# Order edges in a fused decoder step: attention outputs ahead of the output projection's second half, memory and keys turned later

## The chip, the cores and the metric

The kernel runs on one core of a Trainium2 chip. The metric is device time of one execution in microseconds (us). Before the change the median of three runs is 2836.79 us (2836.49 to 2840.41).

Five engines work side by side, each through a list of instructions of its own, in order: TensorE (PE in the profile; its weight loads are PEld), VectorE (DVE), ScalarE (ACT), GpSimd (POOL) and SyncE (SP), which here only issues transfers. They wait for each other by semaphores. A profile also records the clock that TensorE was granted, as a share of full speed (PEclk).

## The reference, cut to what matters

One layer over 2048 prompt tokens of width 1024, and beside it 8 sequences of 4 new tokens. A mixer joins gated linear attention (4 heads) with a spatial gating unit, then come a cross-attention to 256 memory tokens and a gated feed-forward part with a causal convolution; each has an RMS norm ahead and a residual add behind.

```python
def gla_chunked(q, k, v, logg, s0):            # chunks of the sequence
    b = jnp.cumsum(gc, axis=1)
    o = scores @ vc + (qc * jnp.exp(b)) @ S    # outputs: within the chunk, and from the state
    S = jnp.exp(b_last) * S + (kc * jnp.exp(b_last - b)).T @ vc

def mixer(xn, s0, lp):
    ...
    o, S = gla_chunked(q, k, v, logg, s0)
    o = rmsnorm(o, g_gla_out).reshape(B, T, GLA_WIDTH) * jax.nn.silu(r)
    s_out = u * z                              # the gating unit: z mixes positions of sv
    y = jnp.concatenate([o, s_out], axis=-1) @ w_out

def mem_kv(mem, g_mem, wk_x, wv_x):
    mn = rmsnorm(mem, g_mem)
    return mn @ wk_x, mn @ wv_x                # both are outputs too

h = x + mixer(...); h = h + mem_attend(...); out = rmsnorm(h + conv_ffn(...), g_final)
```

(Abridged and partly in short notation.)

## The kernel before, in words

The prompt is worked through in four blocks of 512 tokens, 0 to 3; the new tokens ride along with block 1 in the mixer and with block 2 in the feed-forward part. Products in float32 precision are made from three matmuls (`mm3`: high by high, high by low, low by high), for which every operand is split into a high part (ACT, L84) and a low part (DVE, L85; POOL for some). In names, `h_` and `l_` are the parts of a weight, `ch` and `cl` those of the mixer's output, `r_` a raw weight.

Ahead of block 0 lies the memory stage. `mem_proj` multiplies the normed memory with the key weights and then the value weights, head by head (`mkp`, `mvp`), scales the result into `mkf`/`mvf` on DVE (L568), and at once turns it on TensorE (`mkt`, `mvt`, L577) to store it. Into this stage are woven the turns of block 0's input (`xt`) and of the convolution's state (`sctp`, from transfers `sc`).

In each block, gated linear attention works on two pairs of heads. `decay(p)` makes the decayed keys `kh` (the last step on POOL, L1082) and turns them (`ktp`, L1085); `states(p)` makes the chunk's products `kv` (L1104) and the running state `S` (DVE, L1111); `chunks(p, i)` makes the outputs: `op` (L1127 and L1128, two matmuls per head and chunk, so four for a pair and chunk), copied by DVE (L1129) into `o` for chunk c of 128 tokens. Then, for each c, `onorm(c)` squares (ACT, L1173), sums (DVE, L1174), multiplies by r (L1176) and takes the root through `rt` (DVE, L307) and `ors` (POOL, L308), and `gate(c)` scales (DVE, L1181). `back(h)` turns the result (`otp`, L1187) and splits it into `ch` (ACT, L88) and `cl` (DVE, L89).

The output projection takes eight inputs k: 0 to 3 are linear attention, 4 to 7 the gating unit. With `whole` (blocks 0, 2 and 3) the half over inputs 4 to 7 is made first, for output tiles m = 0 to 3, and these four sums stay open in PSUM as `a_wo`; the matmuls over inputs 0 to 3 follow once `back` is done. Each step of `out_proj_steps` holds two tiles m; the second open step is m = 2 and 3. Block 1 has no open sums.

In block 0 weights are also folded (`qk_steps`, `vo_steps`): `fold_vo` makes `vop` on TensorE and its parts `voh` (ACT) and `vol` (DVE), and stores them for later blocks. `weave` spreads such side steps over steps a to b of the main line; `vo_steps` have (11, 19).

At the very end `last_rows` makes the last rows of the feed-forward part (`dr`), adds them to `ht`, sums squares, and `finish(c, ss)` scales chunk c and stores it; `finish` runs one chunk behind.

What sets the order: the program is written as steps, and a scheduler then sorts each engine's instructions from their dependencies and a model of their times, so an instruction can end up ahead of others that were written before it. A manual dependency of the kind NoSync adds no semaphore; it only keeps one instruction behind another on an engine.

Of the kernel before, what the change touches and what calls it, by code (L numbers as in the profile page):

```python
# [23 lines left out]
SB = 512  # L24
# [13 lines left out]
def hymba_step_kernel(  # L38
# [34 lines left out]
    def mps(name):  # L73
        return mmp.tile([128, 512], F32, tag="mm", name=name)
# [12 lines left out]
    def split_scaled(hi, lo, src, g):  # L87
        act.activation(hi, src, AF.Copy, scale=g)  # L88
        dve.scalar_tensor_tensor(lo, src, g, hi.bitcast(F32), ALU.mult, ALU.subtract)  # L89

    def mm3(ps, wh, wl, xh, xl, first, last):
        pe.matmul(ps, wh, xh, start=first, stop=False)  # L92
        pe.matmul(ps, wh, xl, start=False, stop=False)  # L93
        pe.matmul(ps, wl, xh, start=False, stop=last)  # L94

    def wraw(name):
# [430 lines left out]
    def mem_norm():  # L527
# [27 lines left out]
        mem_st.rs, mem_st.bc = rs, bc  # L555
        mem_st.out, mem_st.t = {}, {}

    def mem_proj(nm, h, od, *ws):

# [10 lines left out]
        for x, t in enumerate((th, tl)):  # L570
            nc.sync.dma_start(kvd[nm, h][:, x], t[:, :512].bitcast(F32))
        if h % 2 == 0:
            mem_st.out[nm] = [U(f"m{nm}o{h}{c}") for c in range(2)]
# [87 lines left out]
    for nm, w, od in (("k", wk_x, o_mem_k), ("v", wv_x, o_mem_v)):  # L661
        od = od[0, 0].rearrange("m h d -> m (h d)")
        for h in range(4):
            mem_steps.append(Step(lambda a, b, nm=nm, h=h, od=od: mem_proj(nm, h, od, a, b),
                                  [(w[0], 4 * j, 4, h * 256, 256, f"w{nm}{h}{j}") for j in range(2)]))
# [278 lines left out]
    def gla_steps(B):  # L944
# [6 lines left out]
        def gates():  # L951
# [24 lines left out]
            B.lg = lg  # L976
            B.P, B.qz, B.kt, B.eb, B.kms, B.b, B.S = {}, {}, {}, {}, {}, {}, {}

# [31 lines left out]
        def level(p, l):  # L1010
# [41 lines left out]
            if sample and l < 2:  # L1052
# [3 lines left out]
                for hh in range(2):  # L1056
                    dst = B.P[2 * p + hh][:NS, SB:TM].rearrange("p (n two h) -> p n two h", two=2, h=half)
                    dve.copy_predicated(dst[:, :, 1, :], masks[l][:NS, :16].rearrange("p (n h) -> p n h", h=half),
                                        ps[:NS, hh * 16:(hh + 1) * 16].rearrange("p (n h) -> p n h", h=half))

        def decay(p):
            e0 = T_(f"e0{s}{p}")
# [19 lines left out]
            pool.tensor_tensor(kh[:, :T], kh[:, :T], B.k[p][:, :T], ALU.mult)  # L1082
            ps = mps(f"ktp{s}{p}")
            for c in range(4):
                pe.transpose(ps[:, c * 128:(c + 1) * 128], kh[:, c * 128:(c + 1) * 128], ident)  # L1085
            t = U(f"kt{s}{p}")
            dve.tensor_copy(t[:, :SB], ps)
            B.kt[p] = t
            if sample:
# [8 lines left out]
        def states(p):  # L1098

            kv = mps(f"kv{s}{p}")  # L1100
            for c in range(4):
# [14 lines left out]
        def chunks(p, i):  # L1116

            if p == 0 and i == 0:
                B.o = [U(f"o{s}{c}") for c in range(nt)]
            ps = mps(f"op{s}{p}{i}")  # L1120
            for j in range(2):
                c = 2 * i + j
                cs = slice(c * 128, (c + 1) * 128)
                for hh in range(2):
                    h = 2 * p + hh
                    os_ = slice(j * 256 + hh * 128, j * 256 + (hh + 1) * 128)
                    pe.matmul(ps[:, os_], B.P[h][:, cs], B.v[c][:, h * 128:(h + 1) * 128], start=True, stop=False)  # L1127
                    pe.matmul(ps[:, os_], B.qz[h][:, cs], B.S[p][c], start=False, stop=True)  # L1128
                dve.tensor_copy(B.o[c][:, p * 256:(p + 1) * 256], ps[:, j * 256:(j + 1) * 256])  # L1129
# [81 lines left out]
    def out_proj_steps(B, unit, src, g, name, sample, first, finished, keep=None, seven=False,  # L1211
# [11 lines left out]
        def half(m2, k0, last, begin=True, end=True):  # L1223

            def fn(wu):
                wh, wl = wu
                x = src()
                if m2 == 0 and last:
                    B.hn, B.sq = [], None
                for mm in range(2):  # L1230
                    m = 2 * m2 + mm
                    ms = slice(mm * 128, (mm + 1) * 128)
                    for ci, (c0, cw) in enumerate(chunks_of(sample)):
                        cs = slice(c0, c0 + cw)
                        ps = acc(f"a_{name}{s}{k0}{m}{ci}") if begin else open_.pop(m)
                        for k in range(4):
                            mm3(ps[:, :cw], wh[:, k, ms], wl[:, k, ms], x[k0 + k][0][:, cs], x[k0 + k][1][:, cs],
                                begin and k == 0, end and k == 3)
                        if end:
# [280 lines left out]
    def ffn_steps(B, last=False):  # L1520
# [110 lines left out]
        def last_rows(*ws):  # L1631
# [8 lines left out]
            def finish(c, ss):  # L1640
                for j in range(2):
# [3 lines left out]
                    else:  # L1645
                        dve.scalar_tensor_tensor(y[:, :512], cur["ht", c, j][:, :512], ss[:, 3:4], gfin[j][:, :512],
                                                 ALU.mult, ALU.mult)
                    nc.sync.dma_start(y_prompt[0, s * SB + c * 128:s * SB + (c + 1) * 128, j * 512:(j + 1) * 512], y[:, :512])

            ready = None  # L1650
            for c in range(4):
                cs = slice(c * 128, (c + 1) * 128)
                ss = narrow(f"yss{s}{c}")
                for j in range(2):
# [6 lines left out]
                    if (c, j) == (3, 1):  # L1661
                        cur["free"], y = y, U("htl")
                        cur["ht", c, j] = y
                        dve.tensor_tensor(y[:, :512], ps, cur["free"][:, :512], ALU.add)
                    else:
# [104 lines left out]
    for s, B in enumerate(blocks):  # L1770
# [6 lines left out]
        if B.mix_sample:  # L1777
            def keep():
                if not hasattr(smp, "x"):
# [63 lines left out]
```

## Time and profile before

| what | us |
|---|---|
| median of 3 runs | 2836.79 |
| the profiled execution | 2837.18 |
| its span | 2835.5 |
| TensorE busy in it | 2797.1 (99%) |
| DVE, ACT, POOL busy | 1894.6, 1106.0, 569.5 |
| mean granted clock of TensorE | 0.995 |
| largest wait of TensorE: otp for the gated o (3 times) | 5.8 |

TensorE is busy nearly throughout. What an order can change is read from the waits of that one engine, from the clock that it had around them, and from the timeline of the other engines just ahead of each wait. In the timeline a row is: start, length, engine, line, operation, output and inputs, count, and in brackets the idle time ahead of it with what ended it.

### The profile page before, as it was taken

How to read it: one execution, taken by the hardware profiler on the slowest of the kernel's cores; microseconds unless marked ns; L12 is line 12 of the kernel's file. 1: busy time of each engine (PE TensorE's matmuls, PEld its weight loads, DVE VectorE, ACT ScalarE, POOL GpSimd, SP SyncE). 2: the span in 40 equal slices, each digit the busy share in tenths (PEclk: the TensorE clock that was granted, in tenths of full speed). 3: DMA queues.
4: the chain of work that ended last, by engine and by line, in shares of the span. 5: the costliest groups of instructions: out<-in, count | busy, mean ns of one | idle time of the engine just before them, and what ended most of it. 6: DMA issues, size and time to landing. Idle time of an engine off the chain costs nothing.

```text
span 2835.5 us, 47052 instructions
## 1 busy us (share of the span) xinstructions
PE 2797.1 (99%) x17894; PEld 2477.9 (87%) x17894; DVE 1894.6 (67%) x3266; ACT 1106.0 (39%) x1950; POOL 569.5 (20%) x638
## 2 busy tenths in 40 slices
PE   8999999999999999999999999999999999999998
PEld 8888888888887898898888889899999888899997
DVE  6578778777657786655555778666666687665555
ACT  5645544333363354223124445422223544431222
POOL 2002213111111221322210121222221022132222
PEclk9999999999999999999999999999999999999999
DMA  9756589999932245888995216577776323677774
GB/s 297 250 182 219 180 267 341 336 343 329 337 112 68 85 154 195 314 288 291 331 324 190 82 60 208 194 252 258 258 269 207 112 69 128 206 260 273 272 281 177
DMA packets 369687, 638.21 MB, mean 225 GB/s; under 512 B 27370, under 2 KB 238412, under 8 KB 369462
## 3 DMA queue, kind: packets, MB, share of 16 engines
q1 hardware_dynamic: 369462, 635.20, 65.7%
q8 instruction: 142, 2.33, 0.3%
q14 instruction: 83, 0.68, 0.1%
HBM read 507.69 MB, written 127.41 MB: 224 GB/s over the span
## 4 chain that ended last, share of the span: by engine, by line
PE 63%; DVE 3%; ACT 1%; issue 0%; POOL 0%; DMA 0%; POOLq 0%; DVEq 0%; ACTq 0%
PE d L94 4%; PE d L92 4%; PE d L93 4%; PE a_wx L94 2%; PE a_wx L93 2%; PE a_wx L92 2%; PE a_wo L92 1%; PE s L1046 1%; PE a_wo L93 1%; PE a_wo L94 1%; PE a_wu L92 1%; PE a_wu L93 1%; PE t_wr L92 1%; PE t_wr L93 1%; PE a_wu L94 1%; PE t_wr L94 1%
## 5 line engine op out<-in xcount | busy, mean ns | idle before, releaser
L92 PE MATMUL d<-acth,whi_wd 128*128 128x272 f32 (+1 forms) x688 | 235.4, 342 | 0.0
L1692 DVE TENSOR_TENSOR h<-d,h 128x512 f32<-128x512 f32 (+1 forms) x232 | 133.7, 582 | 149.4 <-PE d L94 149.2
L94 PE MATMUL d<-acth,wlo_wd 128*128 128x272 f32 (+1 forms) x688 | 233.4, 340 | 0.0
L93 PE MATMUL d<-actl,whi_wd 128*128 128x272 f32 (+1 forms) x688 | 233.3, 339 | 0.0
L1589 POOL TENSOR_TENSOR c<-c,bc_f 128x512 f32<-128x512 f32 (+1 forms) x88 | 137.0, 1562 | 140.4 <-ACT c L1588 139.7
L1579 ACT ACTIVATE c<-g,colsb 128x512 f32<-128x512 f32 x88 | 71.7, 815 | 189.7 <-DVE g L1542 141.7
L94 PEld LDWEIGHTS d<-acth,wlo_wd 128*128 128x128 f32 x688 | 129.5, 188 | 15.5 <-issue 1.2
L93 PEld LDWEIGHTS d<-actl,whi_wd 128*128 128x128 f32 x688 | 129.5, 188 | 13.5 <-issue 0.4
L92 PEld LDWEIGHTS d<-acth,whi_wd 128*128 128x128 f32 x688 | 129.6, 188 | 13.1
L1611 POOL TENSOR_TENSOR c<-r_q_wup,c 128x512 f32<-128x512 f32 (+1 forms) x33 | 63.3, 1918 | 329.4 <-DVE r_q_wup L288 209.6
L92 PE MATMUL a_wo<-ch,h_wo 128*128 128x512 f32 (+1 forms) x320 | 114.3, 369 | 2.0 <-ACT r L876 1.3
L1576 POOL COPY carry<-g 128x2 f32<-128x2 f32 x88 | 29.5, 335 | 420.8 <-DVE g L1542 418.8
L93 PE MATMUL a_wo<-cl,h_wo 128*128 128x512 f32 (+1 forms) x320 | 113.8, 358 | 0.0
L94 PE MATMUL a_wo<-ch,l_wo 128*128 128x512 f32 (+1 forms) x320 | 112.9, 356 | 0.0
L1580 DVE SCALAR_TENSOR_TENSOR c<-g,colsb,c 128x512 f32<-128x512 f32 x88 | 84.9, 965 | 28.3 <-ACT c L1579 27.8
L94 PE MATMUL a_wx<-pTh,wlo_wx 128*128 128x512 f32 x256 | 101.3, 396 | 0.0
L93 PE MATMUL a_wx<-pTl,whi_wx 128*128 128x512 f32 x256 | 100.6, 393 | 0.0
L92 PE MATMUL a_wx<-pTh,whi_wx 128*128 128x512 f32 x256 | 100.2, 394 | 0.0
L84 ACT ACTIVATE acth<-c 128x512 fp32r<-128x512 f32 (+1 forms) x88 | 55.9, 637 | 109.6 <-DVE c L1611 78.0
L1588 ACT ACTIVATE c<-c 128x512 f32<-128x512 f32 (+1 forms) x88 | 56.1, 637 | 94.5 <-DVE c L1581 82.6
L1581 DVE SCALAR_TENSOR_TENSOR c<-g,colsb,c 128x512 f32<-128x512 f32 x88 | 90.6, 1029 | 1.1
L85 DVE TENSOR_TENSOR actl<-c,acth 128x512 fp32r<-128x512 f32 (+1 forms) x88 | 63.1, 720 | 26.6 <-ACT acth L84 25.6
(3753 smaller groups left out, 9741.8 us busy)
## 6 DMA issues: line engine op xcount, KB each, us to landing
whi_wd<-wd SPq DMA_DIRECT2D x66, 512.0 KB, 7.7
wlo_wd<-wd SPq DMA_DIRECT2D x66, 512.0 KB, 7.3
r_wo<-in_w_out_dram SPq DMA_DIRECT2D x32, 512.0 KB, 3.4
wlo_wx<-vod SPq DMA_DIRECT2D x32, 512.0 KB, 4.2
whi_wx<-vod SPq DMA_DIRECT2D x32, 512.0 KB, 5.0
r_wg<-in_w_gate_dram SPq DMA_DIRECT2D x22, 512.0 KB, 7.6
r_wup<-in_w_up_dram SPq DMA_DIRECT2D x22, 512.0 KB, 5.3
r_wd<-in_w_down_dram SPq DMA_DIRECT2D x22, 512.0 KB, 4.5
```

The costliest lines, as they stand in the source:

```text
L84: act.activation(hi, src, AF.Copy)
L85: (lo_eng or dve).tensor_tensor(lo, src, hi.bitcast(F32), ALU.subtract)
L92: pe.matmul(ps, wh, xh, start=first, stop=False)
L93: pe.matmul(ps, wh, xl, start=False, stop=False)
L94: pe.matmul(ps, wl, xh, start=False, stop=last)
L1579: act.activation(c[:, :SB], g[:, 2:SB + 2], AF.Identity, bias=cb, scale=w2)
L1580: dve.scalar_tensor_tensor(c[:, :SB], g[:, 1:SB + 1], w1, c[:, :SB], ALU.mult, ALU.add)
L1581: dve.scalar_tensor_tensor(c[:, :SB], g[:, 0:SB], w0, c[:, :SB], ALU.mult, ALU.add)
L1588: act.activation(c[:, :T], c[:, :T], AF.Gelu_apprx_tanh)
L1589: pool.tensor_tensor(c[:, :T], c[:, :T], B.fbc[:, :T], ALU.mult)
L1611: (dve, pool)[i].tensor_tensor(c[:, :T], q[i], c[:, :T], ALU.mult)
L1692: dve.tensor_tensor(B.h[m + mm][:, cs], ps[:, :cw], B.h[m + mm][:, cs], ALU.add)
```

## The change

Five edits, of which none adds or takes away an operation:

1. `mem_turn`: a head's memory product is turned in the step of the next head (the last one in its own).
2. `keys_turned`: for the second pair of block 0 alone the keys are turned in `states` and no longer in `decay`.
3. `behind(B.last_o, mm)`: the first matmul of the second open step (m = 2, first k) stands behind the last `op` matmul written before it.
4. `behind(cur["added"], out)`: a scaling by DVE in `finish` stands behind the last add, if that add has been written already.
5. `vo_steps` are woven over (11, 17) in place of (11, 19).

```diff
+    in_turn = mybir.DependencyInfo(mybir.DependencyClass.NoSync, mybir.DependencyReason.DATA)
+    def behind(first, then):
+        tc.add_manual_dep(then.ins, first.ins.name, in_turn, reason="in turn")
+
     def mm3(ps, wh, wl, xh, xl, first, last):
-        pe.matmul(ps, wh, xh, start=first, stop=False)
+        out = pe.matmul(ps, wh, xh, start=first, stop=False)
...
+        return out
...
+    def mem_turn(nm, h, od):
+        tf = mem_st.t.pop(("f", nm, h))
         if h % 2 == 0:
...
+            def one(a, b, nm=nm, h=h, od=od):
+                mem_proj(nm, h, a, b)
+                if mem_st.due:
+                    mem_turn(*mem_st.due)
+                mem_st.due = nm, h, od
+                if (nm, h) == ("v", 3):
+                    mem_turn(*mem_st.due)
...
+        def keys_turned(p):
+            kh = B.kh.pop(p)
+            ps = mps(f"ktp{s}{p}")
+            for c in range(4):
+                pe.transpose(ps[:, c * 128:(c + 1) * 128], kh[:, c * 128:(c + 1) * 128], ident)
+            t = U(f"kt{s}{p}")
+            dve.tensor_copy(t[:, :SB], ps)
+            B.kt[p] = t
...
+            B.kh[p] = kh
+            if s or not p:
+                keys_turned(p)
...
         def states(p):
+            if p in B.kh:
+                keys_turned(p)
...
-                    pe.matmul(ps[:, os_], B.qz[h][:, cs], B.S[p][c], start=False, stop=True)
+                    B.last_o = pe.matmul(ps[:, os_], B.qz[h][:, cs], B.S[p][c], start=False, stop=True)
...
+                            mm = mm3(ps[:, :cw], wh[:, k, ms], wl[:, k, ms], x[k0 + k][0][:, cs], x[k0 + k][1][:, cs],
+                                     begin and k == 0, end and k == 3)
+                            if name == "wo" and not end and (m, k) == (2, 0):
+                                behind(B.last_o, mm)
...
+                        out = dve.scalar_tensor_tensor(y[:, :512], cur["ht", c, j][:, :512], ss[:, 3:4],
+                                                       gfin[j][:, :512], ALU.mult, ALU.mult)
+                        if "added" in cur:
+                            behind(cur["added"], out)
...
-                        dve.tensor_tensor(y[:, :512], ps, cur["free"][:, :512], ALU.add)
+                        cur["added"] = dve.tensor_tensor(y[:, :512], ps, cur["free"][:, :512], ALU.add)
...
-        folds = [(qk_steps, 0, 10), (vo_steps, 11, 19)] if s == 0 else []
+        folds = [(qk_steps, 0, 10), (vo_steps, 11, 17)] if s == 0 else []
```

How the order moves is shown at three places. Where a name has digits, the first is the block (a_wo2430: block 2, inputs from 4, tile 3; o23: block 2, chunk 3; op211: block 2, pair 1, chunks 2 and 3), and a number behind an underscore tells buffers apart. Line numbers are those of each kernel.

First, TensorE in block 2, around the last four `op`. Before, a stretch of its list without gaps:

```order
L92 MATMUL a_wo2430_17221<-ch24_16833,h_wo241_16884 128x512
L93 MATMUL a_wo2430_17221<-cl24_16834,h_wo241_16884 128x512
L94 MATMUL a_wo2430_17221<-ch24_16833,l_wo241_16885 128x512
L92 MATMUL a_wo2430_17221<-ch25_16924,h_wo241_16884 128x512
L1127 MATMUL op211_17125<-v23_16525,P210_16719 128x128
L1128 MATMUL op211_17125<-S21_17108,qz210_16960 128x128
L1127 MATMUL op211_17125<-v23_16525,P211_16724 128x128
L1128 MATMUL op211_17125<-S21_17108,qz211_16962 128x128
L93 MATMUL a_wo2430_17221<-cl25_16925,h_wo241_16884 128x512
L94 MATMUL a_wo2430_17221<-ch25_16924,l_wo241_16885 128x512
```

And now:

```order
L98 MATMUL a_wo2400_17172<-ch27_17095,h_wo240_16765 128x512
L99 MATMUL a_wo2410_17185<-cl26_17084,h_wo240_16765 128x512
L100 MATMUL a_wo2410_17185<-ch26_17083,l_wo240_16766 128x512
L98 MATMUL a_wo2410_17185<-ch27_17095,h_wo240_16765 128x512
L99 MATMUL a_wo2400_17172<-cl27_17096,h_wo240_16765 128x512
L100 MATMUL a_wo2400_17172<-ch27_17095,l_wo240_16766 128x512
L99 MATMUL a_wo2410_17185<-cl27_17096,h_wo240_16765 128x512
L100 MATMUL a_wo2410_17185<-ch27_17095,l_wo240_16766 128x512
L1155 MATMUL op211_17125<-v23_16525,P210_16719 128x128
L1156 MATMUL op211_17125<-S21_17108,qz210_16960 128x128
L1155 MATMUL op211_17125<-v23_16525,P211_16724 128x128
L1156 MATMUL op211_17125<-S21_17108,qz211_16962 128x128
```

All of a_wo2420 and a_wo2430, 24 matmuls, now stand between these `op` and the sixteen `otp`, where 8 stood before; the 16 others stood ahead of them. The seven `op` of the earlier chunks stand 6 a_wo earlier than before. Block 3 moves in the same way.

Second, DVE at the same place, from the reduction of chunk 1 (chunk 2's stands beside it) to the splits of the next weights. Before:

```order
L307 TENSOR_SCALAR rt_17148<-oss2_17136 128x4
L307 TENSOR_SCALAR rt_17155<-oss2_17136 128x4
L85 TENSOR_TENSOR l_wo202_17169<-r_wo202_17166,h_wo202_17168 128x1024
L1181 TENSOR_TENSOR o21_16613<-o21_16613,ors2_17137 128x512
L1129 COPY o23_16615<-op211_17125 128x256
L1181 TENSOR_TENSOR o22_16614<-o22_16614,ors2_17137 128x512
L1174 TENSOR_REDUCE oss2_17136<-osq23_17159 128x4
L1176 TENSOR_TENSOR o23_16615<-o23_16615,r23_17052 128x512
L307 TENSOR_SCALAR rt_17162<-oss2_17136 128x4
L85 TENSOR_TENSOR l_wo243_17205<-r_wo243_17202,h_wo243_17204 128x1024
```

And now:

```order
L314 TENSOR_SCALAR rt_17155<-oss2_17136 128x4
L1157 COPY o23_16615<-op211_17125 128x256
L85 TENSOR_TENSOR l_wo202_17169<-r_wo202_17166,h_wo202_17168 128x1024
L1209 TENSOR_TENSOR o21_16613<-o21_16613,ors2_17137 128x512
L1202 TENSOR_REDUCE oss2_17136<-osq23_17159 128x4
L1204 TENSOR_TENSOR o23_16615<-o23_16615,r23_17052 128x512
L1209 TENSOR_TENSOR o22_16614<-o22_16614,ors2_17137 128x512
L314 TENSOR_SCALAR rt_17162<-oss2_17136 128x4
L1209 TENSOR_TENSOR o23_16615<-o23_16615,ors2_17137 128x512
L85 TENSOR_TENSOR l_wo243_17205<-r_wo243_17202,h_wo243_17204 128x1024
```

The copy of chunk 3 stands ahead of the first split, and its gate ahead of the second; before, that gate came behind it.

Third, DVE in block 0, from the copy of chunk 3 to its gate. Before (the gate of chunk 1 stands just ahead):

```order
L1129 COPY o03_2457<-op011_3171 128x256
L85 TENSOR_TENSOR l_wo002_3287<-r_wo002_3284,h_wo002_3286 128x1024
L1181 TENSOR_TENSOR o02_2456<-o02_2456,ors0_3183 128x512
L1174 TENSOR_REDUCE oss0_3182<-osq03_3205 128x4
L1176 TENSOR_TENSOR o03_2457<-o03_2457,r03_3062 128x512
L85 TENSOR_TENSOR vol310_3330<-vop310_3322,voh310_3329 128x512
L307 TENSOR_SCALAR rt_3208<-oss0_3182 128x4
L85 TENSOR_TENSOR l_wo043_3319<-r_wo043_3316,h_wo043_3318 128x1024
L85 TENSOR_TENSOR vol311_3341<-vop311_3333,voh311_3340 128x512
L1181 TENSOR_TENSOR o03_2457<-o03_2457,ors0_3183 128x512
```

And now, from the second of the three reductions on:

```order
L1202 TENSOR_REDUCE oss0_3218<-osq02_3234 128x4
L1204 TENSOR_TENSOR o02_2456<-o02_2456,r02_3086 128x512
L1202 TENSOR_REDUCE oss0_3218<-osq03_3241 128x4
L1204 TENSOR_TENSOR o03_2457<-o03_2457,r03_3087 128x512
L314 TENSOR_SCALAR rt_3230<-oss0_3218 128x4
L314 TENSOR_SCALAR rt_3237<-oss0_3218 128x4
L314 TENSOR_SCALAR rt_3244<-oss0_3218 128x4
L85 TENSOR_TENSOR l_wo043_3319<-r_wo043_3316,h_wo043_3318 128x1024
L1209 TENSOR_TENSOR o01_2455<-o01_2455,ors0_3219 128x512
L1209 TENSOR_TENSOR o02_2456<-o02_2456,ors0_3219 128x512
L1209 TENSOR_TENSOR o03_2457<-o03_2457,ors0_3219 128x512
```

The gates of chunks 1, 2 and 3 now stand together, behind all norms and the split l_wo043; the last two `vop` units and their `vol` have moved ahead of this stretch. On TensorE `ktp` of pair 1 stands behind twelve `a_wo`, where it stood right behind the `s` matmuls, and two head-turns of `mkt` or `mvt` now stand in one place, a head later. Block 1 and the end of the program keep their order on every engine. POOL keeps its order throughout, and SP's differs only up to the end of block 0.

More of the change, by code (lines that the diff above doesn't have):

```diff
@@ L555, in mem_norm, with mem_proj @@
         mem_st.rs, mem_st.bc = rs, bc
-        mem_st.out, mem_st.t = {}, {}
-    def mem_proj(nm, h, od, *ws):
+        mem_st.out, mem_st.t, mem_st.due = {}, {}, None
+    def mem_proj(nm, h, *ws):
         th, tl, tf = U(f"m{nm}h{h}", F32R), U(f"m{nm}l{h}", F32R), U(f"m{nm}f{h}")
@@ L663, in hymba_step_kernel @@
         for h in range(4):
-            mem_steps.append(Step(lambda a, b, nm=nm, h=h, od=od: mem_proj(nm, h, od, a, b),
+            def one(a, b, nm=nm, h=h, od=od):
[5 more added lines that the diff above has]
+                    mem_turn(*mem_st.due)
+            mem_steps.append(Step(one,
                                   [(w[0], 4 * j, 4, h * 256, 256, f"w{nm}{h}{j}") for j in range(2)]))
@@ L1082, in decay @@
             pool.tensor_tensor(kh[:, :T], kh[:, :T], B.k[p][:, :T], ALU.mult)
[L1083 to L1088, printed above, removed]
+            B.kh[p] = kh
+            if s or not p:
+                keys_turned(p)
             if sample:
@@ L1229, in fn @@
                     B.hn, B.sq = [], None
-                for mm in range(2):
-                    m = 2 * m2 + mm
-                    ms = slice(mm * 128, (mm + 1) * 128)
+                for i in range(2):
+                    m = 2 * m2 + i
+                    ms = slice(i * 128, (i + 1) * 128)
                     for ci, (c0, cw) in enumerate(chunks_of(sample)):
```

7 lines of the change are left out of this document (2 added, 5 removed).

## The prediction

> **What bounds the kernel now.** I read the page's head first, then TensorE's waits, the granted clock by stretches, and the timeline around the waits.
>
> ```profile
> span 2835.5 us, 47052 instructions
> PE 2797.1 (99%) x17894; PEld 2477.9 (87%) x17894; DVE 1894.6 (67%) x3266; ACT 1106.0 (39%) x1950; POOL 569.5 (20%) x638
> ```
>
> TensorE is busy for 2797.1 of 2835.5 us, so order can win at most the 38.4 us in which it is not, plus what it loses to a low clock. The profiled execution took 2837.18 us, 1.7 more than its span and 0.4 above the median of the runs, 2836.79; I sum against the former, and the 0.4 drowns in the range.
>
> ```profile
> PE otp L1187 <- DVE o L1181: 5.8, 3, 2.9
> PE mkt L577 <- DVE mkf L568: 2.4, 2, 1.4
> PE otp L1187 <- DVE vol L85: 2.2, 2, 1.3
> PE ktp L1085 <- POOL kh L1082: 1.8, 1, 1.8
> PE sctp L459 <- DMA sc<-in_state_conv_dram: 0.6, 1, 0.6
> PE s L1046 <- ACT h_wof L84: 0.3, 1, 0.3
> ```
>
> Columns: total, times, longest. The largest entry is otp, the transposes of the linear attention's gated outputs; mkt (memory) and ktp (keys) are the other two that the change names. What the waits do not show is the clock behind them (length of the stretch, then busy time by engine, PEclk before the DMA share):
>
> ```profile
> 289.00:292.00 3.00, 1.89 (x7) 1.09 (x7) 1.41 (x4) 0.73 (x2) 0.98 (x1) 0.66 1.07 390
> 292.00:296.00 4.00, 3.99 (x9) 3.15 (x10) 2.72 (x4) 1.69 (x3) 0.00 (x0) 0.50 0.58 216
> 1685.00:1689.00 4.00, 1.14 (x11) 0.90 (x9) 2.65 (x5) 0.41 (x2) 1.91 (x1) 1.00 0.24 56
> 1689.00:1693.00 4.00, 3.55 (x11) 2.65 (x10) 2.73 (x4) 2.39 (x4) 0.00 (x0) 0.57 0.18 75
> 1693.00:1697.00 4.00, 4.00 (x19) 3.24 (x18) 0.00 (x0) 0.00 (x0) 0.00 (x0) 1.00 0.02 4
> 2352.00:2356.00 4.00, 3.77 (x10) 2.87 (x11) 2.71 (x5) 2.42 (x4) 0.00 (x0) 0.50 0.25 99
> ```
>
> After each of the three otp waits the clock falls to half: 10 or 11 matmuls in 4 us instead of 19. So such a wait costs its length and then some.
>
> **Blocks 2 and 3: the edge from op to a_wo.** This is block 2 before:
>
> ```profile
> 1675.19 1.01 POOL L308 TENSOR_TENSOR ors<-rt,neghalf 128x4 f32<-128x4 f32 x1
> ...
> 1681.53 0.38 PE L1127 MATMUL op<-v,P 128*128 128x128 f32 x2
> ...
> 1683.29 0.42 DVE L1129 COPY o<-op 128x256 f32<-128x256 f32 x1
> ...
> 1684.27 1.47 PE L1187 MATMUL otp<-ident,o 128*128 128x128 f32 x12
> ...
> 1685.74 1.22 DVE L85 TENSOR_TENSOR l_wo<-r_wo,h_wo 128x1024 fp32r<-128x1024 f32 x1
> 1685.91 1.91 POOL L308 TENSOR_TENSOR ors<-rt,neghalf 128x4 f32<-128x4 f32 x1 [2.29 <-DVE rt L307]
> 1687.86 0.69 DVE L1181 TENSOR_TENSOR o<-o,ors 128x512 f32<-128x512 f32 x1 [0.90 <-POOL ors L308]
> 1688.60 0.66 PE L1187 MATMUL otp<-ident,o 128*128 128x128 f32 x4 [2.86 <-DVE o L1181]
> ...
> 1689.71 2.07 PE L92 MATMUL a_wo<-ch,h_wo 128*128 128x512 f32 x4 [0.45 <-ACT ch L88]
> ```
>
> The last four op matmuls start at 1681.53; copy, square, reduction, product, root and gate follow, and the gate ends 7.1 us later. TensorE has only 8 a_wo and 12 otp left to cover this. The change puts 16 a_wo that stood ahead of those op behind them, at 0.23 us a step, so op×4 starts 16 × 0.23 = 3.7 us earlier, at 1677.8. Not all of that arrives. DVE must first finish the norms of chunks 1 and 2, which start only 1.4 us earlier (6 a_wo fewer ahead of their op), and now has one weight split l_wo (1.22) ahead of the gates. Chained with these durations: copy 1679.5, split to 1681.8, gate of chunk 1 to 1683, reduction and product of chunk 3 to 1684, gate of chunk 2, root 1684.4. POOL then takes 1.0 instead of 1.91, since the second split now stands behind the gate, and the row at 1675.19 shows that price where no split runs beside it. The last gate ends near 1686.4, which is 2.2 us earlier. TensorE arrives at 1685.65 as before, since the same work stands ahead, so the wait shrinks from 2.86 to about 0.7: **−2.2**. Of the moved a_wo, those that read the late cl now come some 2 us sooner, but POOL has done its last cl before the root at 1675.19, which stands behind it in POOL's queue: no new wait.
>
> Block 3 has the same rows in the same new order:
>
> ```profile
> 2351.34 0.69 DVE L1181 TENSOR_TENSOR o<-o,ors 128x512 f32<-128x512 f32 x1 [0.90 <-POOL ors L308]
> 2352.09 1.11 PE L1187 MATMUL otp<-ident,o 128*128 128x128 f32 x4 [2.77 <-DVE o L1181]
> 2353.34 2.08 PE L92 MATMUL a_wo<-ch,h_wo 128*128 128x512 f32 x4
> ...
> 2358.20 0.50 PE L94 MATMUL a_wo<-ch,l_wo 128*128 128x512 f32 x1
> 2358.54 0.39 PE L92 MATMUL a_wo<-ch,h_wo 128*128 128x512 f32 x1
> ```
>
> Another −2.2 there. Now the clock. Idle pieces summed within about 4 us: 2.9, 2.8 and, in block 0, 2.5 brought half clock; 2.2 (at s and ktp) and 1.4 (mkt) did not. The change leaves 0.7 at otp and 0.45 at a_wo, some 1.2, so I take it that the low clock goes. What it cost is half of its length: from 1689.7 to 1692.8, **−1.55**; from 2353.3 to 2358.4 half of 5.1, and otp×4 at 0.66 instead of 1.11, together **−3.0**. Bounds of these two: 0 and −4.55.
>
> Blocks 2 and 3 together: −2.2 −1.55 −2.2 −3.0 = **−8.95**, between −4.4 (clock still falls) and −11 (waits gone altogether, 1.3 more, and a_wo's too).
>
> **Block 0, keys of the pair.**
>
> ```profile
> 254.44 0.66 PE L1085 MATMUL ktp<-ident,kh 128*128 128x128 f32 x4 [1.83 <-POOL kh L1082]
> ```
>
> These transposes move behind twelve a_wo; 36 vop and the zp of the gating already follow them, so TensorE has work, and kh is ready ten us before its new place: **−1.8**. Eight a_wo (1.8 us) stand between ktp and kv, which cover the copy of kt (about 0.7). The 0.35 at s next to it may go or stay; I count 0.
>
> **Block 0, output projection.**
>
> ```profile
> 268.41 2.67 POOL L85 TENSOR_TENSOR cl<-z,ch 128x512 fp32r<-128x512 f32 x2 [0.79 <-DMA vod<-vol]
> ...
> 286.21 0.82 PE L1187 MATMUL otp<-ident,o 128*128 128x128 f32 x6
> 287.97 0.55 PE L1187 MATMUL otp<-ident,o 128*128 128x128 f32 x3 [0.94 <-DVE vol L85]
> 289.77 0.78 PE L1187 MATMUL otp<-ident,o 128*128 128x128 f32 x3 [1.25 <-DVE vol L85]
> 290.76 1.11 PE L1187 MATMUL otp<-ident,o 128*128 128x128 f32 x4 [0.21 <-DVE o L1181]
> 292.01 2.08 PE L92 MATMUL a_wo<-ch,h_wo 128*128 128x512 f32 x4
> ```
>
> Here I expect a loss. The folds of the value weights end two units earlier, so that 12 vop matmuls leave the stretch between the first a_wo and otp (they are done before it; that alone is worth nothing), and with them its cover. Two waits follow. a_wo meets cl after 14 rows, about 3.8 us after its start, while POOL ends the first cl some 4.9 after it: about 1.0 new. Then DVE has a split, a vol, three reductions and products, and another split ahead of the three gates that remain; chained by the durations above, the second gate ends some 24 us after the first a_wo, TensorE arrives at 20.5: about 3.4. Against 2.4 of waits before that is +2.0; with the switches around it and a clock that still falls (3.4 is more than the 2.5 that sufficed), **+2.8**. Bounds: −5.5, if the waits (2.4) and the half clock (292.0 to 296.8, half of it 2.4, and 0.7 on otp) all go; +4, if the clock stays low for one more stretch of 3.4.
>
> **Memory stage.**
>
> ```profile
> 27.82 0.44 PE L577 MATMUL mkt<-ident,mkf 128*128 128x128 f32 x2 [1.38 <-DVE mkf L568]
> ...
> 34.50 0.41 PE L577 MATMUL mkt<-ident,mkf 128*128 128x128 f32 x2 [1.03 <-DVE mkf L568]
> 63.48 0.29 PE L459 MATMUL sctp<-ident,sc 16*128 16x16 f32 x2 [0.59 <-DMA sc<-in_state_conv_dram]
> ```
>
> Turning each head's product one head later takes away what waited for its evacuation: −2.4 at most. The first wait I expect to stay in part, as DVE holds the evacuation behind a weight split whose weights arrive late, and whatever stops there stops the next head's matmuls too: **−1.2**. In return the transposes of the convolution state come some 4 us sooner, and their last transfer is late already by 0.59; that wait can grow to about 4, the bound on this side. This stage waits for transfers, so either way the gain can be eaten.
>
> **Tail.** The last add's edge changes nothing: every engine keeps its order there. The scalings that would have to wait are issued before the add exists, and the others stood behind it already.
>
> ```profile
> 2825.07 2.41 DVE L1646 SCALAR_TENSOR_TENSOR y<-ht,yss,gf 128x512 f32<-128x512 f32 x2
> ...
> 2827.47 0.68 DVE L1664 TENSOR_TENSOR htl<-dr,ht 128x512 f32<-128x512 f32 x1
> ```
>
> The add at 2827.47 stays behind 2.41 us of scalings: **0**. Had the edge worked, about 1.7 would have been won.
>
> Sum: −8.95 −1.8 +2.8 −1.2 = −9.2. From 2837.18 that gives 2828.0; with the 0.4 down to the median, **2827.6 us**.
>
> **Rivals.**
>
> *The clock still falls in blocks 2 and 3.* For it: about 1.2 of idle in two pieces is left, and block 0's fall came from pieces, none over 1.25. Against it: 2.2 at s and ktp brought none. Then −4.4 −1.8 +2.8 −1.2 = −4.6: 2832. Chance 0.17.
>
> *Block 0 gains too.* For it: the gates of chunks 1 to 3 are now in otp's order. Against it: they are all behind the second split. Then −8.95 −1.8 −5.5 −1.2 = −17.5: 2819.5. Chance 0.15.
>
> *The clock stays up in block 0, though its waits stay.* For it: 1.83 in one piece, at ktp, brought no fall. Against it: 2.5 in four pieces did at this very place. Then −9.2 less the 2.4 and 0.7 of the low clock: −12.3, or 2824.5. Chance 0.05. The Trainium skill, "TensorE: Matmul & The Clock Gate" (What's actually happening), lets the clock fall after an idle window of some 3.4 us that runs free of the program; by that rule this would be the forecast, for a wait of 3.4 seldom fills such a window and shorter ones never do. The rows disagree: 2.86 and 2.77 were followed by half clock.
>
> *The front pays more than the rest wins.* One mechanism: the state's transposes, placed ahead of the value projection, stand first in TensorE's line and wait for a transfer that SP's queue brings after weights; everything up to block 0 waits with them, and the clock, half after such an idle, doubles the next 3.4 us. For it: the 0.59. Against it: only the last of 22 was late. It decides from 9 us on; with 10 of wait, two low stretches (3.4) and block 0's +4 in place of +2.8: −9.2 +10 +3.4 +1.2 = +5.4, so 2842. Chance 0.07.
>
> *Nothing but the order changes*, and the waits reappear at a_wo or the gates of the same blocks: within 2 us of before, 2836. What speaks against it is that the chain from op to otp starts earlier while TensorE's work stays. Chance 0.09.
>
> **How the numbers follow.** My forecast has 0.47, the rivals, in their order, 0.17, 0.15, 0.05, 0.07 and 0.09. Alone, it spans 2824 to 2831 (the bounds of block 0 and the front, half of each). The range to hold 8 of 10 takes in both clock cases and most of block 0's gain: 2819 to 2836. A change under 0.2%, 5.7 us, cannot be told from none: faster is below 2831.1, slower above 2842.5. Faster: the forecast nearly whole (0.44), the second and third rivals (0.20), a third of the first (0.06): 0.70. Same: 0.24. Slower: 0.06.
>
> **What would show it.** In the profile of the changed kernel: otp's waits for the gate in blocks 2 and 3 under 1.2 us each, and PEclk at 1.00 in the 4 us behind them; op×4 some 3.7 us ahead; no ktp wait; one mkt wait instead of two; a wait of a_wo for POOL's cl and one of about 3.4 at otp in block 0, with half clock behind it; the tail unchanged. The forecast is wrong if half clock still follows the otp of blocks 2 and 3, or if block 0 shows no fall of the clock, or if a wait of several us stands before 100 us.

## The result, and the profile after

The changed kernel takes 2832.07 us in the median (2827.63 to 2835.47), beside runs of the kernel before with a median of 2835.41 (one of those 22 runs, of 7065.73, is left out of the ratio). The ratio is 0.9987, 95% interval 0.9981 to 0.9993: some 3.7 us faster, 2.0 to 5.4 by the interval. That is clear of zero, within 0.2% and not the 9.2 that were forecast. The profiled execution shows the same, a span of 2832.4 against 2835.5. First its head and TensorE's waits:

```profile
span 2832.4 us, 47045 instructions
PE 2794.1 (99%) x17894; PEld 2475.0 (87%) x17894; DVE 1893.4 (67%) x3266; ACT 1105.7 (39%) x1950; POOL 572.7 (20%) x638
```

```profile
PE sctp L466 <- DMA sc<-in_state_conv_dram: 3.1, 1, 3.1
PE otp L1215 <- DVE o L1209: 3.0, 3, 2.3
...
PE s L1066 <- DVE kr L1056: 1.2, 1, 1.2
PE s L1066 <- ACT h_wof L84: 1.2, 1, 1.2
...
PE xt L798 <- ACT h L804: 1.1, 1, 1.1
PE mkt L589 <- DVE mkf L575: 1.0, 1, 1.0
...
PE a_wo L99 <- POOL cl L85: 0.8, 1, 0.8
```

The names of before are there, but otp's 5.8 and 2.2 have become 3.0, and ktp's 1.8 is gone. In their place stand waits that before did not have, or had smaller: sctp (0.6 before), s (0.3), a_wo for cl (none). All of them lie ahead of 310 us. The granted clock by stretches says the same (PEclk stands ahead of the DMA share):

```profile
60.00:64.00 4.00, 3.16 (x16) 3.12 (x17) 3.17 (x9) 1.49 (x5) 1.44 (x8) 0.50 1.07 368
...
257.00:261.00 4.00, 2.72 (x15) 2.59 (x16) 3.52 (x8) 2.82 (x5) 0.40 (x1) 0.79 0.27 92
...
298.00:302.00 4.00, 3.86 (x10) 2.78 (x10) 2.73 (x4) 2.24 (x4) 0.00 (x0) 0.50 0.02 4
...
1690.00:1694.00 4.00, 3.55 (x20) 2.85 (x19) 3.88 (x5) 2.45 (x5) 0.00 (x0) 1.00 0.41 123
...
2353.00:2357.00 4.00, 4.00 (x19) 3.24 (x18) 1.86 (x3) 0.84 (x2) 0.00 (x0) 1.00 0.40 131
```

Half clock has left blocks 2 and 3 and has come at 60 and at 260, where before had full clock:

```profile
60.00:64.00 4.00, 3.41 (x30) 3.15 (x29) 2.79 (x7) 1.44 (x2) 0.00 (x0) 1.00 1.07 392
...
257.00:261.00 4.00, 4.00 (x19) 3.32 (x18) 3.29 (x5) 2.55 (x5) 0.00 (x0) 1.00 0.91 291
```

Block 2 in the timeline, the stretch that the prediction worked out:

```profile
1688.20 1.01 POOL L315 TENSOR_TENSOR ors<-rt,neghalf 128x4 f32<-128x4 f32 x1 [1.09 <-DVE rt L314]
...
1689.24 0.69 DVE L1209 TENSOR_TENSOR o<-o,ors 128x512 f32<-128x512 f32 x1 [1.12 <-POOL ors L315]
...
1689.00 1.91 PE L1215 MATMUL otp<-ident,o 128*128 128x128 f32 x16
1691.36 1.20 PE L98 MATMUL a_wo<-ch,h_wo 128*128 128x512 f32 x4 [0.45 <-ACT ch L88]
```

All sixteen otp run in one piece: the last gate ends while TensorE turns the first twelve. POOL's root takes 1.01 and not 1.91, as the split no longer runs beside it. Only a_wo's 0.45 is left.

To see where time went, the start of one instruction at each border (the first `bp` of block 0, at 145.85 before; the first `t_wv` of block 1, 849.79; the first `t_wr` of blocks 2 and 3, 1638.47 and 2302.03) is compared between two traces. Differences to the profile of before, in us, worked out from those starts, for the changed kernel and the experiments below (named by their edits):

| kernel | up to bp | block 0 | block 1 | block 2 | block 3, to the end | sum |
|---|---|---|---|---|---|---|
| changed | +3.5 | +2.7 | −1.4 | −2.9 | −4.9 | −3.1 |
| edge in blocks 2, 3 | −0.3 | +0.6 | −1.4 | −4.5 | −4.9 | −10.4 |
| edge in blocks 0, 2, 3 | +2.4 | −5.0 | −0.2 | −4.9 | −5.1 | −12.7 |
| the same again | −1.0 | −3.6 | −2.3 | −4.4 | −5.1 | −16.4 |
| memory alone | +5.2 | −0.6 | −1.2 | −0.6 | −0.8 | +2.0 |
| folds alone | +1.9 | +7.9 | −2.0 | 0.0 | +2.3 | +10.2 |
| keys alone | +2.1 | +2.7 | −2.1 | +0.9 | +0.7 | +4.4 |
| edge and keys | −0.4 | −2.6 | −1.3 | −4.7 | −4.8 | −13.7 |
| changed, folds as before | +3.1 | −3.8 | −1.0 | −4.7 | −5.0 | −11.3 |
| changed, no edge in block 0 | +1.6 | +3.9 | −2.1 | −3.4 | −5.0 | −5.0 |
| memory, constants later | −3.0 | +0.2 | +1.1 | −0.3 | +0.3 | −1.6 |
| edge, keys, add ahead | +3.4 | −1.1 | −1.0 | −4.7 | −5.9 | −9.3 |
| edge, add ahead | −0.1 | −3.1 | −2.5 | −4.9 | −6.2 | −16.8 |

One profile carries chance: block 1, whose order no edit touches, lies between −2.5 and +1.1. Much of that is the clock: in block 1 the traces have 6.8 us of half clock before, in the first run of the edge in blocks 0, 2 and 3 and in the memory with later constants, and 3.4 us in all others, which is 1.7 us less time lost. In the changed kernel's block 2, the output projection has −4.6, and 1.7 is lost later, most of it at one place where the order is the old one:

```profile
2178.54 0.40 PE L98 MATMUL d<-acth,whi_wd 128*128 128x272 f32 x1 [1.02 <-DVE h L1724]
```

Therefore every verdict below is the ratio of timed runs, and the table only tells where to look.

### The profile page after: what moved, and what is told of

It reads as the page before. It is cut to its first block, busy times and chain, and to the rows that moved or that the text cites. A ratio compares the mean times of both kernels' runs of the same rounds, so it can differ in the third digit from the quotient of the medians.

```text
span 2832.4 us, 47045 instructions
## 1 busy us (share of the span) xinstructions
PE 2794.1 (99%) x17894; PEld 2475.0 (87%) x17894; DVE 1893.4 (67%) x3266; ACT 1105.7 (39%) x1950; POOL 572.7 (20%) x638
## 3 DMA queue, kind: packets, MB, share of 16 engines
q8 instruction: 142, 2.33, 0.3%
## 4 chain that ended last, share of the span: by engine, by line
PE 63%; DVE 3%; DMA 1%; ACT 1%; issue 0%; POOL 0%; POOLq 0%; DVEq 0%; ACTq 0%
PE d L98 4%; PE d L100 4%; PE d L99 4%; PE a_wx L99 2%; PE a_wx L100 2%; PE a_wx L98 2%; PE a_wo L98 1%; PE a_wo L99 1%; PE a_wo L100 1%; PE s L1066 1%; PE a_wu L98 1%; PE a_wu L99 1%; PE t_wr L98 1%; PE a_wu L100 1%; PE t_wr L99 1%; PE t_wr L100 1%
```

## The experiments

The theory after the result: blocks 2 and 3 gain what was forecast, and the memory's turn, the keys and the earlier folds give most of it back ahead of 310 us. The rival: the gain in blocks 2 and 3 itself is not stable, and the rest is chance of the transfers. Four of the five edits were run alone (the tail's changes no order), and two parts of the change, the folds and the edge in block 0, were taken back alone. Each kernel's ratio is to runs of the kernel before on the same chip.

**The edge in blocks 2 and 3 alone.** The memory's turns, the keys and the folds are as before.

```diff
-                            if name == "wo" and not end and (m, k) == (2, 0):
+                            if s and name == "wo" and not end and (m, k) == (2, 0):
```

> Before, plus the edge from op to a_wo in blocks 2 and 3 alone (memory, keys, folds and block 0 as before). Theory 1 (what blocks 2 and 3 gain is given back ahead of 310 us): these two blocks give what the changed kernel showed there, 4.7 and 5.2, so 9.9 us less than before, ratio about 0.9965; no half clock at 1690 and 2353, front and block 0 as before. Theory 2 (the gain in blocks 2 and 3 hangs on when they are reached, or is given back later in them): less than 5 us.

2825.83 us, ratio 0.9964 (0.9950 to 0.9977): 10.2 us less, the 9.9 of theory 1. The rival is out: the gain is there and stays when nothing else is changed.

**The memory's turn alone.** Only `mem_turn` of the change is kept.

> Before, plus the memory's turn one head later alone. Theory 1a: the state's transposes come sooner and wait some 3 us for their last transfer with half clock behind, so the stage ends about 3 us later than before; ratio about 1.001. Theory 1b (the wait seen in the profile of the changed kernel is chance of the transfers): the two waits for mkf shrink from 2.4 to about 1, and the kernel is 1 to 2 us faster or the same.

2839.21 us, ratio 1.0011 (1.0002 to 1.0020): 3.1 us more. The edit that was to win 1.2 loses. TensorE's waits in this run:

```profile
PE sctp L466 <- DMA sc<-in_state_conv_dram: 2.5, 1, 2.5
...
PE mkt L589 <- DVE mkf L575: 1.3, 1, 1.3
PE xt L798 <- ACT h L804: 1.2, 1, 1.2
```

A wait has come at xt, one place on, and sctp's has grown. That mkt's falls from 2.4 to 1.3 is not shown to be the edit's work: in the nine profiles of kernels without it, before among them, mkt's waits come to anything from 0.6 to 2.5 (with it, to 1.3 at most). At the other two places the profiles do tell the kernels apart. Without the edit sctp waits 1.5 at most and xt not at all; in the four profiles with it and the constants where they were, sctp waits 2.1 to 3.4 and xt 0.4 to 1.5.

**The folds over steps 11 to 17 alone.**

```diff
-        folds = [(qk_steps, 0, 10), (vo_steps, 11, 19)] if s == 0 else []
+        folds = [(qk_steps, 0, 10), (vo_steps, 11, 17)] if s == 0 else []
```

> Before, plus the folds of the value weights over steps 11 to 17 alone. Theory 1c: the two waits at the last s matmuls (for kr on DVE, 1.2, and for h_wof on ACT, 1.2) and the half clock at 259 to 262 come from this edit: they appear here too, and block 0's otp lose cover; 3 to 5 us more than before, ratio about 1.0015. Theory 1d (they come from the keys or the edge): no wait for kr, no half clock before 280; within 1 us of before up to the first a_wo.

2842.99 us, ratio 1.0025 (1.0015 to 1.0035): 7.1 us more, past the 3 to 5 of theory 1c. This smallest of the edits is the dearest:

```profile
PE otp L1210 <- DVE o L1204: 9.4, 4, 2.9
...
PE s L1062 <- DVE kr L1052: 2.4, 2, 1.2
...
PE ktp L1081 <- POOL kh L1107: 2.3, 1, 2.3
```

The two waits at s come with this edit, and otp's grow from 8.0 (5.8 and 2.2) to 9.4, since 12 vop no longer stand between the last op and otp. In the changed kernel the rows behind the waits at s are these:

```profile
251.15 0.74 DVE L939 SCALAR_TENSOR_TENSOR z<-zp,colsb,bsb 128x512 f32<-128x512 f32 x1
...
252.41 2.32 DVE L85 TENSOR_TENSOR l_wo<-r_wo,h_wo 128x1024 fp32r<-128x1024 f32 x1
254.66 1.51 DVE L1060 TENSOR_TENSOR e<-e,k 128x256 f32<-128x256 f32 x1
256.09 0.87 DVE L1056 SCALAR_TENSOR_TENSOR kr<-e,sel,q 128x256 f32<-128x256 f32 x2
```

And before:

```profile
242.73 0.74 DVE L919 SCALAR_TENSOR_TENSOR z<-zp,colsb,bsb 128x512 f32<-128x512 f32 x1
...
246.57 1.91 DVE L1036 SCALAR_TENSOR_TENSOR kr<-e,sel,q 128x256 f32<-128x256 f32 x2
```

`kr` feeds s. DVE's way to it has not changed: z, e, a split, e and two kr stand in the same order, and from the start of z to the end of the second kr it is 5.8 us in both. What is shorter is TensorE's way. Between zp, from which DVE makes z, and s it has 22 `t_wr` matmuls where 34 stood before, both in the folds alone and in the changed kernel; at 0.23 each that is 2.8 us of cover less. So TensorE gets to s at 255.9, before the first kr is done.

**The edge in blocks 0, 2 and 3 alone.** All else as before.

> Before, plus the edge from op to a_wo in blocks 0, 2 and 3. Against the run with blocks 2 and 3 alone it tells what the edge does in block 0. Theory 1e: with the folds where they were (12 vop behind the last op as cover) the edge helps block 0 too, and its otp waits of 2.5 and half clock shrink: 2 to 5 us less than with blocks 2 and 3 alone, ratio about 0.9955. Theory 1f: cl of the gating unit is then awaited by a_wo and block 0 loses 1 to 3 us.

2824.49 us, ratio 0.9954 (0.9942 to 0.9967). It was run once more later:

> The run with the edge in blocks 0, 2 and 3 alone once more, beside the others of this call: ratio 0.9945 to 0.9965, no half clock between 280 and 300, at 1690 or at 2353. Its stage ahead of 150 us may differ from the first time by up to 3 us, if the transfers there scatter as the profiles so far suggest.

2823.86 us, ratio 0.9958 (0.9946 to 0.9970). The intervals overlap that of blocks 2 and 3 alone, so the times leave a gain of 1 to 3 us in block 0 likely and not proven; the trace shows it plainly. TensorE in block 0:

```profile
288.55 1.14 PE L1210 MATMUL otp<-ident,o 128*128 128x128 f32 x9
290.13 0.55 PE L1210 MATMUL otp<-ident,o 128*128 128x128 f32 x3 [0.43 <-DVE o L1204]
291.24 1.19 PE L98 MATMUL a_wo<-ch,h_wo 128*128 128x512 f32 x4 [0.56 <-ACT ch L88]
```

Before, 2.4 us were lost at this place and half clock followed; here 0.43 and 0.56, and full clock. Block 0 is 5.0 and 3.6 shorter in the two profiles. So theory 1e holds where the folds stay late.

**The folds taken back, all else as changed.**

> The changed kernel with the folds back over steps 11 to 19, all else as changed. Theory 1c (the folds' window costs 7 us, as it did alone): no wait of s for kr, no half clock at 260, block 0's otp nearly without a wait; 7 us below the changed kernel, so about 10 to 11 below before, ratio about 0.9963. Theory 3 (the turned keys bring the waits at s): the waits at s stay and the ratio is 0.998 or more.

2827.59 us, ratio 0.9976 (0.9967 to 0.9985). The waits at s fall to 0.43, and otp's to 1.2. Against the changed kernel's 0.9987 that is 3 us, not the 7 of the edit alone: with the edge in block 0 the cover of the folds is worth less. The profiles have 6.5 in block 0 (+2.7 against −3.8); the timed runs say less, and the size stays between.

**The edge and the keys.**

> Before, plus the edge in blocks 0, 2 and 3 and the keys of the pair turned later; memory and folds as before. The wait of ktp (1.83) goes and, with it, some half clock that follows it where the window falls so: 2 to 3 us less than with the edge alone, 13 to 14 below before, ratio about 0.9952. If instead the later keys make kv late, a wait at kv or op of 1 to 2 us appears and the ratio is that of the edge alone, 0.9954 or above 0.996.

2826.07 us, ratio 0.9971 (0.9959 to 0.9983): not below the edge alone, rather above. The gain of 1.8 isn't there. So the keys were run alone as well:

> Before, plus the keys of the pair turned later alone. Theory 4a (the wait only moves): with the keys 19 a_wo later the wait of ktp (1.83) is gone, but kv and all op come later, and what is lost reappears as longer waits at otp with half clock behind; 0 to 4 us above before, ratio 1.0 to 1.0015. Theory 4b (the wait is won, as predicted): 2 us below before, ratio about 0.9993.

2838.91 us, ratio 1.0009 (1.0000 to 1.0017): 2.6 us more, theory 4a. ktp waits no more, and otp pays:

```profile
PE otp L1211 <- DVE o L1205: 7.5, 4, 2.8
PE otp L1211 <- DVE vol L85: 3.5, 2, 2.1
```

Together 11.0 against 8.0 before, with half clock behind: 3.0 more, for 1.8 saved. Counted from the first `bp`, TensorE now reaches otp 1.4 us sooner, but kv and the first op after it come 3.8 us later and the four gates 2.7 to 7.1 later. This run does not have the order of the changed kernel, however: alone, the edit puts ktp behind nineteen a_wo, with 23 more ahead of kv; there, and with the edge, it is twelve and eight. With the edge, two new waits of about 0.8, at a_wo for cl and at otp, take back most of what ktp gave, and block 0 is 2.6 shorter than before where the edge alone had 5.0 and 3.6. The timed runs put the loss beside the edge at some 4 us (0.9971 against 0.9954 and 0.9958); as these intervals overlap, its size stays open.

**The changed kernel without the edge in block 0.**

> The changed kernel without the edge in block 0 (blocks 2 and 3 keep it). Theory 5a (the folds' window alone takes block 0's cover, and the edge helps there even so): 3 to 5 us above the changed kernel, at about the time before, ratio 1.0. Theory 5b (with the folds early the edge in block 0 itself does the harm): 1 to 3 us below the changed kernel, ratio 0.9975 to 0.9985.

2835.86 us, ratio 1.0000 (0.9991 to 1.0009): 3.7 us more than the changed kernel, theory 5a. The folds and the keys have taken all cover from otp:

```profile
296.89 3.06 PE L1215 MATMUL otp<-ident,o 128*128 128x128 f32 x12 [6.28 <-DVE o L1209]
```

**The memory's turn with the late constants two steps later.**

```diff
-    steps += weave(mem_steps, (norm, 0, 11), ([Step(late_constants)], 2, 2))
+    steps += weave(mem_steps, (norm, 0, 11), ([Step(late_constants)], 4, 4))
```

> Before, plus the memory's turn one head later, with the late constants (and the turns of the convolution's state behind them) two steps later than before. Theory 2a (what the turn costs is that these turns came ahead of their transfer): no wait at sctp and no half clock at 60; 0 to 2 us below before, ratio 0.9993 to 1.0. Theory 2b (the order of the memory turns themselves, or the transfers, cost it): still 2 to 4 us above before, ratio about 1.001.

2836.49 us, ratio 1.0008 (0.9999 to 1.0017). Both theories lose a part. There is no wait at sctp any more, and full clock up to 280 us, but the timed runs are not faster than before, nor told apart from 1.0011. That sctp is the whole of what the memory's turn costs is therefore not shown; xt's 1.2 is still there, and the rest stays open.

**A last add that does stand ahead.** The scalings of chunk 1 are written behind the adds of chunk 3, so that the edge has something to hold:

```diff
-                if ready:
-                    finish(*ready)
-                ready = c, ss
-            finish(*ready)
+                ready.append((c, ss))
+                if c != 2:
+                    for r in ready[:-1]:
+                        finish(*r)
+                    del ready[:-1]
+            finish(*ready[0])
```

> As the run of edge and keys, plus a last add that really stands ahead: the scalings of chunk 1 are written behind the adds of chunk 3, so that the edge has something to hold. The add starts some 1.6 us sooner, but the sum of squares' add then stands behind four scalings (2.8 us): from TensorE's end to the last instruction 0.5 to 1.0 us less than the 9.66 of before. By the other reading (the end hangs on the stores alone) no change there.

2825.29 us, ratio 0.9967 (0.9956 to 0.9978), and from TensorE's end to the last instruction 8.6 us against 9.66, a little more than the 0.5 to 1.0 less that I expected. The same on top of the edge alone, the best of all kernels here:

> The edge in blocks 0, 2 and 3 and the last add ahead of the scalings of chunks 1 and 2 in the program as well: as the run beside it less 1.1 us at the end (8.6 from TensorE's end to the last instruction, as in the run with keys, against 9.66); ratio about 0.0004 lower, 0.994 to 0.996. If the tail gives nothing, the same ratio.

2821.56 us, ratio 0.9948 (0.9935 to 0.9961): 14.7 us less than before, 11 below the changed kernel. Its tail:

```profile
2810.13 0.69 DVE L1691 TENSOR_TENSOR htl<-dr,ht 128x512 f32<-128x512 f32 x1 [0.45 <-PE dr L100]
2810.74 2.07 DVE L1671 SCALAR_TENSOR_TENSOR y<-ht,yss,gf 128x512 f32<-128x512 f32 x3
2812.72 0.74 DVE L1671 SCALAR_TENSOR_TENSOR ht<-ht,yss,gf 128x512 f32<-128x512 f32 x1
...
2814.38 0.75 DVE L1671 SCALAR_TENSOR_TENSOR y<-htl,yss,gf 128x512 f32<-128x512 f32 x1 [0.66 <-POOL yss L315]
```

The add now starts as soon as TensorE is through, 1.6 us sooner against TensorE's end, and four scalings behind it cost 0.5 of that. In time the 1.1 is below what these runs tell apart (0.9948 against 0.9958); the trace has it in both kernels.

## Why the prediction was right and where it was not

The range (2819 to 2836) holds the time, and the direction is right. The sum is not: −9.2 forecast, −3.7 measured, and "within 0.2%", to which I gave 0.24, is what came. That the range holds is in part luck: two terms have the wrong sign and a cost is missing in a third, and together they happened to stay below what blocks 2 and 3 won. That the time equals the 2832 of the first rival is luck too, as its half clock in blocks 2 and 3 did not come. By its terms:

**Blocks 2 and 3, −8.95: right.** The edge alone gives −10.2 (−14.2 to −6.5). The chain from op to otp, POOL's 1.0 in place of 1.91, no new wait at cl, and the clock all came as worked out; op×4 start 3.65 us earlier, counted from the block's start, where I had 3.7. The last gate ended 1.2 us sooner than I had it, counted in the same way, so that the wait went whole instead of to 0.7. The price of the clock was read from one profile, and it varies: half clock lasts 3.4 us in block 2 and 6.8 in block 3 before, 6.8 and 3.4 with the keys alone, and with the memory alone block 2 has none, after the same waits of 2.8 to 2.9.

**The tail, 0: right.** The waits and the order there are those of before; from TensorE's end to the last instruction it is 9.67 (9.66). When the add was really put ahead, 1.1 was won and not the 1.7 that I named: the scalings were moved and not removed.

**Keys, −1.8: wrong.** The step that failed is "these transposes move behind twelve a_wo …, so TensorE has work". That is so, and it isn't enough: I followed ktp to kv and its copy, and not on to op, onorm, gate and otp, the chain that I had just used for the edge and that ends last here. Alone, in an order that puts the keys later still, the edit costs 2.6; beside the edge, with the twelve a_wo of the changed kernel, some 4.

**Block 0's output projection, +2.8: the right size there.** In the changed kernel:

```profile
276.87 0.50 PE L99 MATMUL a_wo<-cl,h_wo 128*128 128x512 f32 x1 [0.76 <-POOL cl L85]
...
292.41 0.60 PE L1215 MATMUL otp<-ident,o 128*128 128x128 f32 x4
295.34 0.66 PE L1215 MATMUL otp<-ident,o 128*128 128x128 f32 x4 [2.33 <-DVE o L1209]
296.33 0.68 PE L1215 MATMUL otp<-ident,o 128*128 128x128 f32 x4 [0.33 <-DVE o L1209]
297.30 1.11 PE L1215 MATMUL otp<-ident,o 128*128 128x128 f32 x4 [0.30 <-DVE o L1209]
```

0.76 where I had 1.0, and 2.96 in three pieces where I had 3.4, with half clock behind, as forecast. What is wrong is a sentence in its working: that the 12 vop "are done before it; that alone is worth nothing". With the folds earlier, TensorE has twelve t_wr less between zp and s and waits there for DVE's kr and ACT's h_wof, which costs 2.4 (0.3 before) and a stretch of half clock. That is the earlier folds' other half, which I priced at zero without looking at who waits on DVE and ACT there.

**Memory, −1.2: the wrong sign.** One mkt wait is left, of 1.0, as I said; but the 2.4 from which I took my price was one value out of 0.6 to 2.5 that kernels without the edit show. The row of sctp, late by 0.59 already, and the 4 us by which its transposes come sooner were both on my page; together they give a wait of several us, and I put that at the bound and took −1.2. In the profile it is 3.07, with half clock behind it, and so one of my own signs of a wrong forecast, a wait of several us before 100 us, is there. This is the mechanism of the rival in which the front pays, at a third of its price. Alone, the edit costs 3.1 (0.6 to 5.7).

Four kernels build the change up part by part, and so the runs give its sum: the edge in blocks 0, 2 and 3 has −13.0 and −11.9 in its two runs (0.9954 and 0.9958), with the keys it is −8.2 (0.9971), with the memory as well −6.8 (0.9976) and with the folds −3.7 (0.9987). So the keys take back some 4, the memory 1 to 2 and the folds 3. Neighbouring intervals overlap, so which of the three costs most is not shown; that together they take back most of the gain is. The costs differ from those of each edit alone (2.6, 3.1 and 7.1). For keys and folds that is no surprise, as both live on the same cover, TensorE's work ahead of otp: with both and without the edge in block 0, the wait there is 6.28.

The rival in which half clock stays in blocks 2 and 3 is out in every run with the edge. The one in which block 0 gains too is what the profiles show without the folds' edit (−3.8 there). The one in which block 0 keeps its waits but not its half clock did not come: PEclk is 0.50 from 298 to 302.

## What to carry to other kernels

An order edge that starts a long chain sooner is worth its wait and the low clock behind it, if the work that it moves can stand behind the chain's start. Before moving anything else ahead or back near such a chain, ask which cover it takes: follow each moved piece to the last instruction that hangs on it, and look at what the other engines have in line where it arrives. Edits that are each worth a few us are to be run one by one, and then one on top of the other, since their costs need not add up; here one of five carried the gain, three gave most of it back, and one did nothing until the program itself was written in the other order.

## What the runs showed of the hardware

**The same idle time is followed by half clock in some executions and not in others.** Kernels whose order up to there is the same wait 0.35 at s and 1.83 at ktp near 253 us in each of their profiles. With the edge in blocks 2 and 3:

```profile
254.00:256.00 2.00, 1.96 (x9) 1.63 (x10) 2.00 (x5) 0.00 (x0) 0.00 (x0) 0.83 0.00 0
256.00:258.00 2.00, 2.00 (x6) 1.60 (x5) 1.76 (x4) 0.60 (x1) 0.00 (x0) 0.50 0.47 130
```

And in the best kernel:

```profile
254.00:256.00 2.00, 1.69 (x10) 1.47 (x11) 2.00 (x5) 0.00 (x0) 0.26 (x1) 1.00 0.00 0
256.00:258.00 2.00, 2.00 (x10) 1.66 (x9) 1.93 (x5) 0.84 (x2) 0.00 (x0) 1.00 0.32 89
```

So my reading, that 2.5 us of idle bring the fall and 2.2 do not, was a line drawn through chance: 2.2 can bring it. The edge and keys, without and with the added tail, show it for 1.8 (0.77, 0.44 and 0.56 within 3 us near 290): 1.00 from 290 to 298 in the one, down to 0.50 in the other. A single 0.45, in blocks 2 and 3, was never followed by it. Nor does a long gap always bring it: with the memory alone, block 2 keeps full clock after 2.85 in one piece. Ahead of the program's last stretch, half clock lasts 3.41, 6.83 or 10.24 us in all profiles here, so one fall costs half of that, 1.7 us or a multiple. The Trainium skill, "TensorE: Matmul & The Clock Gate" (What's actually happening), says that the monitor's window runs free of the program, and the scatter agrees with that; its idle window of some 3.4 us does not fit as a lower limit for one gap, since falls here came with gaps of 2.77 in one piece, of 1.8 in pieces and, in block 1 with the folds alone, of 1.75 in one piece that ends at 1040.8 (half clock from 1041.8).

**The stage that waits for transfers scatters by 4 us with one order.** Eight profiles of kernels with the same order up to the first bp reach it between 1.0 us sooner and 3.4 us later than the profile of before. A single pair of profiles cannot price an edit there.

**Where work of DVE and POOL overlaps, the one that starts second can take longer.** POOL's root of 128x4 took 1.91 where it started 0.17 after DVE's split (which kept its 1.22) and 1.01 without a split. The other way round, in the changed kernel, POOL has these two running

```profile
251.97 1.68 POOL L949 TENSOR_TENSOR z<-z,u 128x512 f32<-128x512 f32 x1 [13.87 <-DVE z L939]
254.39 1.50 POOL L85 TENSOR_TENSOR cl<-z,ch 128x512 fp32r<-128x512 f32 x1 [0.74 <-ACT ch L84]
```

while DVE's split l_wo, which starts at 252.41 with z under way, takes 2.32 and ends 1.08 after z, and its product e at 254.66 takes 1.51 (0.43 at 258.04). In the profiles of before and after, all seven splits `l_wo` and `l_wof` that start within 0.5 us after a z take 2.31 to 2.33 and end 1.07 to 1.08 after it. It is not so for every overlap: a split that starts 0.36 after a root, at 985.26 before, takes 1.20. Both slow rows lie in the chain that TensorE waits for at s; they are no new cost of the change, as that chain has a split of 2.32, at 243.99, before as well.
